# Second feed-forward product of a two-layer trunk: one chain for its loads, moved residual rows, earlier statistics

## The chip, the cores and the metric

One core of a Trainium2 chip runs the whole program. The metric is the device time in microseconds (us) of one execution; several runs are taken and their median is used. The engines are TensorE (PE in the profile; PEld is its weight load), VectorE (DVE), ScalarE (ACT), GpSimd (POOL) and SyncE (SP, which issues nearly all DMA transfers).

## The reference

Two layers; each has a token mixer (latent attention in layer 0, RWKV-7 in layer 1) with memory attention beside it, and then a squared-ReLU feed-forward block:

```
x = layer_norm(ALPHA * x + mix, ln1_g[i], ln1_b[i])
ff = square(relu(x @ w_ff1[i])) @ w_ff2[i]          # 1024x1024 @ 1024x4096, then @ 4096x1024
x = layer_norm(ALPHA * x + ff, ln2_g[i], ln2_b[i])
```

All of it is f32 with 1024 tokens of width 1024. The change lies in the product with `w_ff2` and in the last `layer_norm`.

## The kernel before, in words

Each f32 operand is split into a high part (ScalarE, line 143) and a low part (VectorE, line 144), and each product is three matmuls of 128x128 by 128x512: high-high, high-low, low-high. Both feed-forward products use a Strassen-Winograd scheme: matrices are cut into quarters, and seven smaller products are taken of quarters and their sums and differences. The first product (in `out_and_ff`) writes the hidden quarters A11, A12, A22 and the sums S1 to S4 to DRAM (`h_d`, line 1480), 128 rows per block p = 0..15. It keeps the operand T4 in a pool on the right side of SBUF (lines 1464 and 1465) until its last matmuls.

`second_product` (line 1554) reads them back with the quarters of `w_ff2` in five stretches:

1. A11 x B11 into the PSUM tiles X (`ps_y`) and A12 x B21 into Y (`ps_z`). Steps 0 and 1 hold one block p each and take both weight quarters in one load; steps 2 to 8 hold two blocks (p = 2, 4, ... 14) and need four loads of 512 KB: A11, B11, A12, B21. B21 goes to the kept tile `D_` (`dka` for p < 8, `dkb` for the rest). A step of two blocks has 48 matmuls.
2. S2 and S1 with sums of weights, two blocks a step, five loads a step (lines 1685 to 1690); three weight sums per step are VectorE's.
3. S4 x B22, two loads a step.
4. S3 with a weight difference, three loads a step.
5. A22 with the weights kept in `D_`, one load a step.

Between them `out` (lines 1636 and 1638) adds PSUM tiles into the residual rows `R`, eight row tiles of 128x1024. Before that each row tile is loaded from `n_d` (line 1677) and scaled by g1 and b1 (`scale_rows`, lines 171 and 172, on VectorE). The vectors g1, b1, g2, b2 are loaded as broadcast rows (line 1583) into the ring of four `slot` tiles, which the first product uses too.

Loads go through a ring of raw buffers: `raw()` (line 138) takes turns among the pools `wr`, `w4`, `w3`, `w5` and `w5` again (two buffers each, four in w5). Step 0 uses one of `wr` and one of `w4`; the first buffer of `w5`, which is opened on the right side (line 1576), goes to step 1's hidden rows.

The order of instructions on each engine is written by a planner, which simulates the program and issues what is ready, in program order among the ready. `issue_after(ins)` adds an order edge to `ins` for those instructions of its block that run on the engine of `ins`; it adds no wait. In the code before, the blocks at lines 1659, 1669 and 1674 name `ms[0]`, a matmul, and contain DMA issues of SyncE and VectorE operations:

```
ms = product(X, A1, B1, fresh, end)
with self.tc.issue_after(ms[0]):
    nc.sync.dma_start(r, n_d[(i - 1) * P : i * P, :])
    self.scale_rows(r, g1, b1, nc.vector, nc.vector)
```

In the last layer each row tile is normalised when its sum is complete (`finish`), scaled by g2 and b2 (`affine`) and stored; row tile 7 is stored in two halves (`last_layernorm`). `cp` is a scratch tile of the first product that is free in the second.

Of the kernel before, what the change touches and what calls it, by code (L numbers as in the profile page):

```python
# [10 lines left out]
F32 = mybir.dt.float32  # L11
# [9 lines left out]
P = 128  # L21
T = 1024
D = 1024
KT = D // P
H = 512
# [41 lines left out]
class Trunk:  # L67
# [103 lines left out]
        (mul or self.nc.gpsimd).tensor_mul(r, r, g)  # L171
        (add or self.nc.gpsimd).tensor_add(r, r, b)

    def normalise(self, r):
        y, t = self.row_scale(r)
        self.nc.scalar.activation(r, r, AF.Identity, scale=y, bias=t)


    def last_layernorm(self, r, g, b, dst):
        nc = self.nc  # L180
        y, t = self.row_scale(r)
        for i, (c, q) in enumerate(((slice(0, H), nc.sync), (slice(H, D), nc.scalar))):
            nc.scalar.activation(r[:, c], r[:, c], AF.Identity, scale=y, bias=t)
            self.scale_rows(r[:, c], g[:, c], b[:, c], nc.vector, nc.vector)
            q.dma_start(dst[:, c], r[:, c])


    def row_scale(self, r):
        nc, sm = self.nc, self.sm
        small = lambda name: sm.tile([P, 2], F32, name=f"ln2_{name}", bufs=2)[:, 0:1]  # L190
        st = sm.tile([P, 2, 2, 6], F32, name="ln2_st", bufs=2)[:, 0]
        mv = sm.tile([P, 2, 2], F32, name="ln2_mv", bufs=2)[:, 0, :]
        for i in range(2):
            nc.vector.bn_stats(st[:, i, :], r[:, i * H : (i + 1) * H])
        nc.vector.bn_aggr(mv, st)
        xh, y, t = small("h"), small("y"), small("t")
        nc.vector.tensor_scalar(t, mv[:, 1:2], 1e-5, None, op0=ALU.add)
        nc.vector.tensor_scalar(xh, t, -0.5, None, op0=ALU.mult)
        nc.vector.tensor_scalar(t.bitcast(I32), t.bitcast(I32), 1, None, op0=ALU.logical_shift_right)
        nc.vector.tensor_scalar(y.bitcast(I32), t.bitcast(I32), -1, 0x5F3759DF, op0=ALU.mult, op1=ALU.add)  # L200
        for _ in range(3):
            nc.vector.scalar_tensor_tensor(t, y, xh, y, op0=ALU.mult, op1=ALU.mult)
            nc.vector.scalar_tensor_tensor(y, t, 1.5, y, op0=ALU.add, op1=ALU.mult)
        nc.vector.scalar_tensor_tensor(t, mv[:, 0:1], -1.0, y, op0=ALU.mult, op1=ALU.mult)
        return y, t
# [1043 lines left out]
    def out_and_ff(self, layer, res_src, res_dst, last, R=None):  # L1249
        nc, a = self.nc, self.a  # L1250
        n_d = self.dp.tile([T, D], F32, name=f"n_d{layer}")

        h_d = self.dp.tile([7 * NFF // 2 * P, H], F32, name=f"h_d{layer}")
        h_rows = lambda k, p, n=1: h_d[(k * NFF // 2 + p) * P : (k * NFF // 2 + p + n) * P, :]
        A11_, A12_, A22_, S1_, S2_, S3_, S4_ = range(7)
        pool_of = lambda st: lambda name, bufs=1, **k: st.enter_context(self.tc.tile_pool(name=f"{name}{layer}", bufs=bufs, reuse_waits="tile", **k))
        wv = a["w_ff1"][layer].rearrange("(k p) f -> p k f", p=P)
        quad = lambda t: t.rearrange("p (a b) -> p a b", b=P)
        T0, T1 = slice(0, H), slice(H, T)
        with ExitStack() as s:  # L1260
            pool = pool_of(s)
            cp = pool("cp").tile([P, 2, H], F32, name="cpair")
            pst = pool("pstr", 2, space=PSUM, side="right")
# [7 lines left out]
            with ExitStack() as s1:  # L1271
# [70 lines left out]
                with ExitStack() as s2:  # L1342
# [47 lines left out]
                    if R is None:  # L1390
                        K1 = self.Xh.t[1], self.Xl.t[1]
                        R = Halves(new(0, F32), new(1, F32))
# [152 lines left out]
                        final(*held)  # L1545
                    held = (p, w, A) + m
                final(*held)
            self.second_product(layer, res_dst, last, n_d, h_rows, s, pool_of, pst, slot)
            self.wrs = [self.wr]

    def second_product(self, layer, res_dst, last, n_d, h_rows, s, pool_of, pst, slot):
        nc, a = self.nc, self.a
        A11_, A12_, A22_, S1_, S2_, S3_, S4_ = range(7)
        pool = pool_of(s)
# [18 lines left out]
        w5 = pool("w5", 4, side="right")  # L1576
        self.wrs, self.rn = [self.wr, w4], 1

        def rows(i):
            out = []  # L1580
            for j in range(2):
                t = slot(F32)
                nc.sync.dma_start(t, a["rows"][i + j : i + j + 1, :].broadcast_to([P, D]))
                out.append(t)
            return out

        def hidden(k, p, n=2):
            t = two(self.raw(), n)
            nc.sync.dma_start(t, h_rows(k, p, n).rearrange("(n p) t -> p n t", p=P))
            return t  # L1590

        def weight(i, j, p, n=2, t=None):
            t = two(self.raw(), n) if t is None else t
            nc.sync.dma_start(t, wv[i][:, p : p + n, j * H : (j + 1) * H])
            return t

        def ring(homes):
            while True:
                yield from homes

        def operand(t, home):
            z = [x[:, : t.shape[1], :] for x in home]
            self.split(*z, t)
            return z
# [15 lines left out]
        def product(ps, A, B, fresh, end):  # L1620
            return [block(ps, t, [(A, B)], fresh, end) for t in range(4)]
# [11 lines left out]
        def out(ps, t, tt, cs, fresh):  # L1633
            r = R[:, tt, cs]
            if fresh:
                nc.vector.scalar_tensor_tensor(r, r, ALPHA, ps[t], op0=ALU.mult, op1=ALU.add)
            else:
                nc.vector.tensor_add(r, r, ps[t])

        steps = range(0, N, 2)  # L1640
        home, gate = ring(full), []

        for i, (p, n) in enumerate([(0, 1), (1, 1)] + [(p, 2) for p in steps[1:]]):
            fresh, end = i == 0, p == steps[-1]
            if n == 1:

                t = two(self.raw())
                for j, k in enumerate((A11_, A12_)):
                    nc.sync.dma_start(t[:, j, :], h_rows(k, p))
                w = two(self.raw())  # L1650
                nc.sync.dma_start(w, a["w_ff2"][layer, 2 * p * P : 2 * (p + 1) * P, c0].rearrange("(i p) d -> p i d", p=P))
                za = operand(t, [two(slot()) for _ in range(2)] if i == 0 else next(home))
                zb = operand(w, [two(x) for x in self.split_pair()])
                (A1, B1), (A2, B2) = ([[x[:, j : j + 1, :] for x in z] for z in (za, zb)] for j in range(2))
            else:
                A1, B1 = operand(hidden(A11_, p), next(home)), operand(weight(0, 0, p), next(home))
                A2, (B2, t) = operand(hidden(A12_, p), next(home)), (next(home), D_(p, 2))

                with self.tc.issue_after(gate.pop(0)):
                    weight(1, 0, p, t=t)  # L1660
                B2 = operand(t, B2)
            ms = product(X, A1, B1, fresh, end)
            gate.append(ms[0])
            if end:
                for t in range(4):
                    out(X, t, t, c0, True)
            product(Y, A2, B2, fresh, end)
            if i == 0:
                with self.tc.issue_after(ms[0]):
                    g1, b1 = rows(4 * layer)  # L1670
                self.wrs = [self.wr, w4, w3, w5, w5]
            else:
                r = R[:, i - 1, :]
                with self.tc.issue_after(ms[0]):
                    if i == 1:
                        weight(1, 0, 0, t=D_(0, 2))
                    nc.sync.dma_start(r, n_d[(i - 1) * P : i * P, :])
                    self.scale_rows(r, g1, b1, nc.vector, nc.vector)
        for t in range(4):
            out(Y, t, t, c0, False)  # L1680

# [1 line left out]
        for p in steps:  # L1683
            end = p == steps[-1]
            t11, t12, t22 = weight(0, 0, p), weight(0, 1, p), weight(1, 1, p)
            nc.vector.tensor_sub(t11, t12, t11)
            nc.vector.tensor_sub(t22, t22, t11)
            A, B = operand(hidden(S2_, p), next(home)), operand(t22, next(home))
            A2, B2 = operand(hidden(S1_, p), next(home)), operand(t11, next(home))
            nc.vector.tensor_sub(D_(p, 2), D_(p, 2), t22)  # L1690
            product(X, A, B, False, end)
            if end:
                for t in range(4):
                    out(X, t, t, c1, True)
            product(Y, A2, B2, p == 0, end)
# [11 lines left out]
        def affine(tt):  # L1707
            self.scale_rows(R[:, tt, :], g2, b2, nc.vector, nc.vector)
            nc.sync.dma_start(res_dst[tt * P : (tt + 1) * P, :], R[:, tt, :])
# [2 lines left out]

        def finish(tt):
            if last and tt == KT - 1:
                self.last_layernorm(R[:, tt, :], g2, b2, res_dst[tt * P : (tt + 1) * P, :])
            elif last:
                self.normalise(R[:, tt, :])
                affine(tt)
            elif tt % 2:
                self.normalise2(pair(tt - 1))  # L1720

# [8 lines left out]
                finish(i - 1)  # L1730
        for t in range(4):
            out(X, t, 4 + t, c1, False)

        k = 2 if last else 6
        ops = []
# [160 lines left out]
```

## Time and profile before

| | |
|---|---|
| runs (3) | 2732.3 us median, 2723.94 to 2739.67 |
| profiled execution | 2742.62 us, span 2740.8 |
| PE busy | 2580.5 us (94%) |
| DVE busy | 1805.5 us (66%) |
| ACT busy | 1264.6 us (46%) |
| granted TensorE clock, mean | 0.967 |
| DMA queue q1 | 359.25 MB, 38.6% of 16 engines' span |

The profiled execution is one run, seen by the hardware profiler; rows of its trace add up to its own time. Busy shares are means over the span. The second product of layer 0 runs from about 885 to 1225 us, that of layer 1 from about 2396 us to the end.

### The profile page before, as it was taken

What the parts mean: (1) busy time and instruction counts of PE and PEld (TensorE: products, weight loads), DVE (VectorE), ACT (ScalarE), POOL (GpSimd) and SP (SyncE); (2) the same over time, 40 slices, a digit from 0 to 9 for tenths busy, and PEclk for the clock granted to TensorE, in tenths of its full rate; (3) what the DMA queues carried; (4) which work ended last, traced back from release to release, by engine and by line L of the source; (5) the groups of instructions that cost most, each with busy time, mean ns of one, the idle gap of its engine ahead of it and who ended that gap; (6) DMA issues with size and microseconds to landing.
All of it is one profiled execution on the core that took longest, in us unless ns stands there. A gap on an engine that the chain in (4) does not pass through costs nothing.

```text
span 2740.8 us, 41038 instructions
## 1 busy us (share of the span) xinstructions
PE 2580.5 (94%) x15709; PEld 2085.7 (76%) x15709; DVE 1805.5 (66%) x3195; ACT 1264.6 (46%) x2242; POOL 428.0 (16%) x703
## 2 busy tenths in 40 slices
PE   8999998999999799999989999888998999979998
PEld 7877776778888588887877777666776888858886
DVE  5566766586656676675356566677769666667677
ACT  4465555254444233357344444666527444423343
POOL 0012232000000000002354453454400000000000
PEclk9999999999999899999999999989999999989999
DMA  4100003235445867535521221213114544486661
GB/s 166 56 28 14 9 20 109 88 108 181 146 150 182 315 209 223 184 125 209 193 85 51 72 76 63 93 48 127 59 51 142 177 150 154 158 331 216 218 233 65
DMA packets 233732, 362.13 MB, mean 132 GB/s; under 512 B 14336, under 2 KB 113024, under 8 KB 233536
## 3 DMA queue, kind: packets, MB, share of 16 engines
q1 hardware_dynamic: 233392, 359.25, 38.6%
q8 instruction: 124, 2.03, 0.3%
q14 instruction: 72, 0.59, 0.1%
q10 hardware_dynamic: 144, 0.26, 0.0%
HBM read 254.86 MB, written 104.60 MB: 131 GB/s over the span
## 4 chain that ended last, share of the span: by engine, by line
PE 79%; DVE 10%; DMA 4%; ACT 3%; issue 2%; POOL 1%; SPq 0%; DVEq 0%; POOLq 0%; ACTq 0%
PE ps_f L1288 20%; PE ps_y L1613 12%; PE ps_z L1613 8%; PE ps_in L149 4%; PE ps_in L150 4%; PE ps_in L151 4%; PE ps_o L645 2%; PE ps_pt L636 2%; PE ps_o L149 2%; PE ps_o L150 2%; PE ps_o L151 2%; PE ps_s L611 1%; PE ps_ga L1036 1%; PE ps_s L613 1%; PE ps_s L612 1%
## 5 line engine op out<-in xcount | busy, mean ns | idle before, releaser
L143 ACT CAST Xh<-wraw 128x1024 fp32r<-128x1024 f32 (+1 forms) x138 | 139.2, 1037 | 238.4 <-PE ps_z L1613 72.0
L149 PE MATMUL ps_in<-Xh,whi 128*128 128x512 f32 x480 | 197.6, 414 | 13.3 <-ACT whi L143 9.4
L150 PE MATMUL ps_in<-Xl,whi 128*128 128x512 f32 x480 | 195.2, 407 | 0.8 <-DVE Xl L144 0.8
L151 PE MATMUL ps_in<-Xh,wlo 128*128 128x512 f32 x480 | 194.2, 405 | 0.0
L144 DVE TENSOR_TENSOR Xh<-wraw,Xh 128x1024 fp32r<-128x1024 f32 x115 | 137.6, 1221 | 57.9 <-ACT Xh L143 57.5
L143 ACT CAST Xl<-wraw 128x1024 fp32r<-128x1024 f32 x103 | 104.8, 1050 | 146.7 <-issue 46.1
L144 DVE TENSOR_TENSOR Xl<-wraw,Xl 128x1024 fp32r<-128x1024 f32 x103 | 123.5, 1220 | 50.0 <-ACT Xl L143 49.5
L144 DVE TENSOR_TENSOR wlo<-wraw,whi 128x1024 fp32r<-128x1024 f32 (+3 forms) x93 | 107.1, 1153 | 65.4 <-ACT whi L143 64.9
L143 ACT CAST whi<-wraw 128x1024 fp32r<-128x1024 f32 (+3 forms) x93 | 88.3, 953 | 105.7 <-PE ps_in L150 37.9
L149 PEld LDWEIGHTS ps_in<-Xh,whi 128*128 128x128 f32 x480 | 93.2, 194 | 35.3 <-ACT whi L143 9.4
L626 POOL TENSOR_TENSOR E<-E,l 128x768 f32<-128x768 f32 (+5 forms) x60 | 83.8, 1399 | 201.6 <-DVE l L624 101.3
L1288 PE MATMUL ps_f<-Xh,N 128*128 128x512 f32 x320 | 106.8, 398 | 4.9 <-ACT N L143 2.1
L695 POOL MEMSET wraw<- 128x1 f32 x2 | 0.2, 98 | 698.0 <-DVE wraw L1727 697.9
L150 PEld LDWEIGHTS ps_in<-Xl,whi 128*128 128x128 f32 x480 | 93.1, 194 | 20.1 <-DVE Xl L144 1.3
L151 PEld LDWEIGHTS ps_in<-Xh,wlo 128*128 128x128 f32 x480 | 92.4, 193 | 20.3 <-issue 1.1
L623 ACT ACTIVATE E<-ps_s,mx,SC 128x128 f32<-128x128 f32 (+7 forms) x96 | 79.4, 831 | 51.0 <-DVE mx L621 24.5
L1288 PE MATMUL ps_f<-TB,N 128*128 128x512 f32 x384 | 91.9, 389 | 0.1
L1613 PE MATMUL ps_y<-Xh 128*128 128x512 f32 x384 | 90.0, 389 | 0.0
L1613 PE MATMUL ps_z<-Xh 128*128 128x512 f32 x384 | 89.6, 389 | 0.0
L1613 PE MATMUL ps_z<-Xl 128*128 128x512 f32 x384 | 89.3, 389 | 0.0
L1613 PE MATMUL ps_y<-Xh,Xh 128*128 128x512 f32 x360 | 85.4, 391 | 0.0
L1288 PEld LDWEIGHTS ps_f<-TB,N 128*128 128x128 f32 x384 | 72.0, 188 | 15.4 <-ACT N L143 0.5
(522 smaller groups left out, 7014.5 us busy)
## 6 DMA issues: line engine op xcount, KB each, us to landing
wraw<-in_w_ff_dram SPq DMA_DIRECT2D x182, 512.0 KB, 4.4
wraw<-h_d SPq DMA_DIRECT2D x108, 512.0 KB, 4.2
h_d<-slot SPq DMA_DIRECT2D x128, 256.0 KB, 2.1
h_d<-tr SPq DMA_DIRECT2D x64, 256.0 KB, 2.0
wraw<-in_w_in_dram SPq DMA_DIRECT2D x31, 512.0 KB, 4.0
lo_d<-l_st SPq DMA_DIRECT2D x36, 256.0 KB, 2.3
rkv_d<-rkv_st SPq DMA_DIRECT2D x36, 256.0 KB, 2.3
rkv<-rkv_d SPq DMA_DIRECT2D x24, 384.0 KB, 3.7
```

Of the source, the lines that this page charges most:

```text
L143: h = self.nc.scalar.copy(hi, src)
L144: l = self.nc.vector.tensor_sub(lo, src, f32(hi))
L149: mm(ps, wh, xh, start=first, stop=False)
L150: mm(ps, wh, xl, start=False, stop=False)
L151: mm(ps, wl, xh, start=False, stop=last)
L611: nc.tensor.matmul(o, qh[:, isl], kh, start=True, stop=False)
L623: nc.scalar.activation(E3[:, g, :], S[:, g * w0 : g * w0 + n], AF.Exp, bias=mx[:, g : g + 1], scale=SC[:, i : i + 1], accum_out=l[:, g : g ...
L626: nc.gpsimd.tensor_mul(E3, E3, l[:, :, None].broadcast_to([P, nh, n]))
L636: nc.tensor.transpose(pt[:, j, :], E3[:, g, (j0 + j) * P : (j0 + j + 1) * P], self.ident)
L645: nc.tensor.matmul(po[64 * hd : 64 * hd + 64, i4 * P : (i4 + 1) * P], V[:, j, (2 * pr + hd) * 64 : (2 * pr + hd + 1) * 64], pts[hd][:, j, ...
L1288: yield nc.tensor.matmul(ps, A[x][:, k, :], B[y][:, k, :], start=fresh and k == 0 and i == 0, stop=k == 3 and i == 2, skip_group_check=True)
L1613: m = nc.tensor.matmul(ps[t], A[x][:, u, t * P : (t + 1) * P], B[y][:, u, :], start=fresh and i == u == j == 0, stop=end and i == last_ an ...
```

## The change

All loads of `second_product` go through a new helper `load`, which queues each behind the load before it, in the order of the program text. The residual rows are loaded and scaled from step 3 of the first stretch on, one per step, and two in the second stretch. The vectors g1 and b1 come after step 2. In the last layer, the statistics of the right halves of row tiles 4 to 7 are taken after the fourth stretch, into `cp`, and row tile 6 is scaled and stored after row tile 7.

```diff
+    def row_scale(self, r, st=None):
...
+        halves = range(2 if st is None else 1)
+        st = sm.tile([P, 2, 2, 6], F32, name="ln2_st", bufs=2)[:, 0] if st is None else st
+        for i in halves:
             nc.vector.bn_stats(st[:, i, :], r[:, i * H : (i + 1) * H])
...
+        queue = [None]
+        def load(dst, src):
+            with ExitStack() as st:
+                if queue[0] is not None:
+                    st.enter_context(self.tc.issue_after(queue[0]))
+                queue[0] = nc.sync.dma_start(dst, src).ins
...
         def hidden(k, p, n=2):
             t = two(self.raw(), n)
-            nc.sync.dma_start(t, h_rows(k, p, n).rearrange("(n p) t -> p n t", p=P))
+            load(t, h_rows(k, p, n).rearrange("(n p) t -> p n t", p=P))
...
+        def residual(t):
+            load(R[:, t, :], n_d[t * P : (t + 1) * P, :])
+            self.scale_rows(R[:, t, :], g1, b1, nc.vector, nc.vector)
...
-                A2, (B2, t) = operand(hidden(A12_, p), next(home)), (next(home), D_(p, 2))
-
-                with self.tc.issue_after(gate.pop(0)):
-                    weight(1, 0, p, t=t)
-                B2 = operand(t, B2)
-            ms = product(X, A1, B1, fresh, end)
-            gate.append(ms[0])
+                A2 = operand(hidden(A12_, p), next(home))
+                B2 = operand(weight(1, 0, p, t=D_(p, 2)), next(home))
+            product(X, A1, B1, fresh, end)
...
             if i == 0:
-                with self.tc.issue_after(ms[0]):
-                    g1, b1 = rows(4 * layer)
                 self.wrs = [self.wr, w4, w3, w5, w5]
-            else:
-                r = R[:, i - 1, :]
-                with self.tc.issue_after(ms[0]):
-                    if i == 1:
-                        weight(1, 0, 0, t=D_(0, 2))
-                    nc.sync.dma_start(r, n_d[(i - 1) * P : i * P, :])
-                    self.scale_rows(r, g1, b1, nc.vector, nc.vector)
+            if i == 2:
+                g1, b1 = rows(4 * layer)
+                weight(1, 0, 0, t=D_(0, 2))
+            if i >= 3:
+                residual(i - 3)
...
             nc.vector.tensor_sub(D_(p, 2), D_(p, 2), t22)
+            if 2 <= p <= 4:
+                residual(5 + p // 2)
...
             if last and tt == KT - 1:
-                self.last_layernorm(R[:, tt, :], g2, b2, res_dst[tt * P : (tt + 1) * P, :])
+
+                self.last_layernorm(R[:, tt, :], g2, b2, res_dst[tt * P : (tt + 1) * P, :], stats[:, 3])
+                affine(tt - 1)
             elif last:
-                self.normalise(R[:, tt, :])
-                affine(tt)
+                self.normalise(R[:, tt, :], stats[:, tt - 4] if tt >= 4 else None)
+                if tt != KT - 2:
+                    affine(tt)
...
+        if last:
+            stats = cp[:, 0, 0:48].rearrange("p (t i s) -> p t i s", t=4, i=2)
+            for t in range(4):
+                nc.vector.bn_stats(stats[:, t, 1, :], R[:, 4 + t, c1])
```

`rows`, `weight` and the two single loads of steps 0 and 1 use `load` in the same way.

## Rows read from the trace of the kernel before

**Rows 1.** Waits of TensorE, whole span: in total, times, longest.

```profile
PE ps_y L1613 <- ACT Xh L143: 31.0, 2, 16.6
```

**Rows 2.** Timeline of TensorE, head of layer 0's second product: start, us, instruction.

```profile
895.75 0.39 PE L1613 MATMUL ps_z<-whi,slot 128*128 128x512 f32 x1
910.57 0.79 PE L1613 MATMUL ps_y<-whi,Xh 128*128 128x512 f32 x1 [14.44 <-ACT Xh L143]
...
936.17 5.69 PE L1613 MATMUL ps_z<-Xl,Xh 128*128 128x512 f32 x16 [1.66 <-DVE Xh L144]
941.70 3.56 PE L1613 MATMUL ps_y<-Xh,Xh 128*128 128x512 f32 x15
```

**Rows 3.** Chain of work that ended last, second stretch of layer 0.

```profile
1001.70 5.44 PE ps_y L1613 x24
...
1023.46 5.44 PE ps_y L1613 x24
```

**Rows 4.** Windows, TensorE alone: length, busy (count), clock, DMA share, GB/s.

```profile
896.10:941.60 45.50, 27.32 (x97) 0.74 0.93 360
2407.10:2446.95 39.85, 21.18 (x81) 0.79 1.00 393
```

**Rows 5.** Timeline of TensorE, head of layer 1's second product.

```profile
2406.76 0.39 PE L1613 MATMUL ps_z<-whi,slot 128*128 128x512 f32 x1
...
2440.21 4.83 PE L1613 MATMUL ps_z<-Xh,Xl 128*128 128x512 f32 x20 [1.73 <-DVE Xh L144]
...
2447.02 3.28 PE L1613 MATMUL ps_z<-Xl,Xh 128*128 128x512 f32 x13 [0.17 <-DVE Xh L144]
```

**Rows 6.** Windows, all engines (PE, PEld, DVE, ACT, POOL), the wait and after.

```profile
896.10:910.60 14.50, 0.06 (x2) 0.03 (x1) 8.88 (x10) 1.04 (x1) 0.00 (x0) 0.60 1.04 412
910.60:918.70 8.10, 8.10 (x24) 6.49 (x25) 3.63 (x3) 3.15 (x3) 0.00 (x0) 0.66 1.04 404
```

**Rows 7.** Timeline of SyncE's queue, layer 0.

```profile
870.95 0.46 SPq L1589 DMA_DIRECT2D wraw<-h_d  x1
...
893.58 5.42 SPq L1677 DMA_DIRECT2D R<-n_d  x5
899.38 1.51 SPq L1649 DMA_DIRECT2D wraw<-h_d  x2
```

**Rows 8.** Landing times of lines 1649, 1651 and 1677, in this order.

```profile
DMA to landing us min/median/max: 2.5/5.8/9.4
...
DMA to landing us min/median/max: 3.6/4.8/6.3
...
DMA to landing us min/median/max: 8.9/9.5/10.7
```

**Rows 9.** Timeline of TensorE, the last reader of T4 in layer 0.

```profile
891.66 0.39 PE L1288 MATMUL ps_f<-T,wlo 128*128 128x512 f32 x1
```

**Rows 10.** Timeline of VectorE and ScalarE, layer 0.

```profile
901.52 0.69 DVE L1531 TENSOR_TENSOR tr<-tr,slot 128x512 f32<-128x512 f32 x1
...
903.22 6.16 DVE L171 TENSOR_TENSOR R<-R,slot 128x1024 f32<-128x1024 f32 x5 [1.01 <-DMA R<-n_d]
...
909.47 1.04 ACT L143 CAST Xh<-wraw 128x1024 fp32r<-128x1024 f32 x1 [15.94 <-DMA wraw<-h_d]
...
913.26 1.23 DVE L144 TENSOR_TENSOR Xl<-wraw,Xl 128x1024 fp32r<-128x1024 f32 x1
```

**Rows 11.** Timeline of VectorE, second stretch of layer 0.

```profile
1026.60 1.22 DVE L1690 TENSOR_TENSOR dkb<-dkb,wraw 128x1024 f32<-128x1024 f32 x1
```

**Rows 12.** Windows, all engines, unbroken part of layer 0's first stretch.

```profile
936.20:1023.30 87.10, 87.10 (x377) 71.99 (x377) 58.54 (x57) 31.13 (x32) 0.00 (x0) 0.98 0.63 199
```

**Rows 13.** Chain of work that ended last, end of the kernel.

```profile
2729.15 1.14 DVE R L171
2730.29 0.60 DVE ln_st L194
2730.89 1.12 DVE R L172
```

More of the change, by code (lines that the diff above doesn't have):

```diff
@@ L172, in scale_rows, with normalise, last_layernorm @@
         (add or self.nc.gpsimd).tensor_add(r, r, b)
-    def normalise(self, r):
-        y, t = self.row_scale(r)
+    def normalise(self, r, st=None):
+        y, t = self.row_scale(r, st)
         self.nc.scalar.activation(r, r, AF.Identity, scale=y, bias=t)
-    def last_layernorm(self, r, g, b, dst):
+    def last_layernorm(self, r, g, b, dst, st):
         nc = self.nc
-        y, t = self.row_scale(r)
+        y, t = self.row_scale(r, st)
         for i, (c, q) in enumerate(((slice(0, H), nc.sync), (slice(H, D), nc.scalar))):
@@ L185, in last_layernorm @@
             q.dma_start(dst[:, c], r[:, c])
-    def row_scale(self, r):
+    def row_scale(self, r, st=None):
         nc, sm = self.nc, self.sm
         small = lambda name: sm.tile([P, 2], F32, name=f"ln2_{name}", bufs=2)[:, 0:1]
-        st = sm.tile([P, 2, 2, 6], F32, name="ln2_st", bufs=2)[:, 0]
         mv = sm.tile([P, 2, 2], F32, name="ln2_mv", bufs=2)[:, 0, :]
-        for i in range(2):
+        halves = range(2 if st is None else 1)
+        st = sm.tile([P, 2, 2, 6], F32, name="ln2_st", bufs=2)[:, 0] if st is None else st
+        for i in halves:
             nc.vector.bn_stats(st[:, i, :], r[:, i * H : (i + 1) * H])
@@ L1547, in out_and_ff, with second_product @@
                 final(*held)
-            self.second_product(layer, res_dst, last, n_d, h_rows, s, pool_of, pst, slot)
+            self.second_product(layer, res_dst, last, n_d, h_rows, s, pool_of, pst, slot, cp)
             self.wrs = [self.wr]
-    def second_product(self, layer, res_dst, last, n_d, h_rows, s, pool_of, pst, slot):
+    def second_product(self, layer, res_dst, last, n_d, h_rows, s, pool_of, pst, slot, cp):
         nc, a = self.nc, self.a
@@ L1582, in rows @@
                 t = slot(F32)
-                nc.sync.dma_start(t, a["rows"][i + j : i + j + 1, :].broadcast_to([P, D]))
+                load(t, a["rows"][i + j : i + j + 1, :].broadcast_to([P, D]))
                 out.append(t)
@@ L1593, in weight @@
             t = two(self.raw(), n) if t is None else t
-            nc.sync.dma_start(t, wv[i][:, p : p + n, j * H : (j + 1) * H])
+            load(t, wv[i][:, p : p + n, j * H : (j + 1) * H])
             return t
+        def residual(t):
+            load(R[:, t, :], n_d[t * P : (t + 1) * P, :])
+            self.scale_rows(R[:, t, :], g1, b1, nc.vector, nc.vector)
         def ring(homes):
@@ L1640, in second_product @@
         steps = range(0, N, 2)
-        home, gate = ring(full), []
+        home = ring(full)
         for i, (p, n) in enumerate([(0, 1), (1, 1)] + [(p, 2) for p in steps[1:]]):
@@ L1648, in second_product @@
                 for j, k in enumerate((A11_, A12_)):
-                    nc.sync.dma_start(t[:, j, :], h_rows(k, p))
+                    load(t[:, j, :], h_rows(k, p))
                 w = two(self.raw())
-                nc.sync.dma_start(w, a["w_ff2"][layer, 2 * p * P : 2 * (p + 1) * P, c0].rearrange("(i p) d -> p i d", p=P))
+                load(w, a["w_ff2"][layer, 2 * p * P : 2 * (p + 1) * P, c0].rearrange("(i p) d -> p i d", p=P))
                 za = operand(t, [two(slot()) for _ in range(2)] if i == 0 else next(home))
```

## The prediction

> **What bounds the kernel now.** TensorE is by far the busiest engine of the page's table, so only its idle or slowed stretches can be won. The list of what TensorE waited for comes first: its longest entry is 31.0 us in two waits, both in the second feed-forward product, behind a ScalarE cast (line 143, the high half of an operand) [rows 1]. No other entry of the list's head lies in code that the change touches. So the question is what happens at the head of that product, once per layer.
>
> TensorE's timeline of layer 0 shows it. The last matmul of step 0 starts at 895.75, the first of step 1 at 910.57; a later piece begins after a gap of 1.66 at 936.17, and from 941.70 on nothing interrupts it [rows 2]. Undisturbed, 24 matmuls take 5.44 us, 0.2267 each [rows 3]. Between 895.98 (895.75 + 0.23) and 941.70, 45.72 us, it did 96 matmuls (the window's x97 counts the one that reaches into it) [rows 2, 4], worth 96 x 0.2267 = 21.76. Lost: 23.96 us. In layer 1 step 0 ends at 2406.99 and the unbroken part begins at 2447.02: 40.03 us for 80 matmuls (x81, counted in the same way) [rows 4, 5], worth 18.13. Lost: 21.90. Together 45.9 us: 31.0 are the two long waits, the rest is lower clock (0.74 and 0.79 were granted over the two stretches [rows 4]) and shorter gaps.
>
> Why is step 1 late? During the wait the DMA engines are full, at 412 GB/s [rows 6], so that 512 KB take 0.524 / 0.41 = 1.28 us of them. SyncE's timeline shows what they carry: hidden rows of step 2 issued at 870.95, five residual rows from 893.58 to 899.0, and only then, at 899.38, the hidden rows that step 1 wants [rows 7]. A residual row takes 9.5 us to land here [rows 8]. By the code these rows should follow a matmul of their own step, ms[0]; but that helper orders only instructions of the named one's engine, and the loads are SyncE's. The trace bears it out: five were issued before step 1's first matmul. The order that the old code asks for was never in force, and the new chain, whose links are all SyncE's, is a real change of order.
>
> **The change part by part, per layer.**
>
> *The chain's first price.* Step 1's hidden rows go to the first buffer of w5, which by the code lies where T4 lay. T4's last reader starts at 891.66 [rows 9], so the buffer is free near 891.9, whatever the order. The loads behind it in the chain, some of which leave at 870 to 892 today, now wait for 892; but then only stores are in front of them. Two halves of hidden rows at 0.32 of SyncE each land 2.5 us after issue at best, the weights 3.6 at best [rows 8]: hidden rows landed 892.1 + 0.3 + 0.64 (half of 1.28) + 2.5 = 895.5, cast (1.04 [rows 10], 1.05 with its start) at 896.6; weights issued by 893.1, landed 896.7, cast 897.8, low half on VectorE (1.23 [rows 10]) 899.0. Step 0 still ends at 895.98, so TensorE idles 3.0 us where it idled 14.6.
>
> *Clock.* After the long wait 24 matmuls took 8.1 us [rows 6] where 5.4 would do: 2.7 lost. After the gap of 1.73 in layer 1, 20 matmuls took 4.83 where 20 x 0.2267 + 0.16 (the last one's tail) = 4.69 would do: 0.14 lost; after layer 0's gap, 16 took 5.53 for 3.63: 1.9 lost [rows 2, 5]. A 3 us gap lies between 0.1 and 2.7; I take 1.5, nearer to the short gaps.
>
> *Step 2.* Its four loads (2 MB) follow directly: the first pair is landed by 896.7 + 2 x 1.28 = 899.3, or 901.2 with three 256 KB stores of the last block between (0.64 each); cast and low half make 903.5. Step 1's 24 matmuls run until 899.0 + 5.44 + 1.5 = 905.9. VectorE also has six sums of the last block (0.69 each [rows 10], 4.1) and four low halves: 892.5 + 4.1 + 4.9 = 901.5. Covered; bounds 0 to 4 us (the six sums on top), I take 1 for VectorE's order.
>
> *Row vectors.* The two of them (1 MB) and one more weight block go behind step 2. The second waits for a slot that the last block's stores leave; today the last of its sums starts at 901.52 [rows 10], so it goes by 904 at the latest and holds back step 3: landed by 904 + 4 x 1.28 + 2.5 = 911.6, wanted at 905.9 + 10.9 = 916.8. Hidden; if not, it costs up to those 2 us of its late issue.
>
> *Residual rows.* Eight loads leave the head of the queue and return one per step from step 3: 2.5 MB per step, 5 x 1.28 = 6.4 us of DMA in a step of 48 matmuls, 10.88. VectorE per step: four low halves, 4.9, and a mul and an add (6.16 / 5 = 1.23 each [rows 10]), 7.4 of 10.88. Two rows fall into the second stretch, where a step already costs VectorE seven such operations, 8.6; with the row 11.1 of 10.88. VectorE's lead covers it: at 1026.60 it works on the first weight block of dkb (p = 8) [rows 11], while TensorE began p = 4 at 1023.46 (two steps after p = 0 at 1001.70) [rows 3]. Without that lead the two rows cost 2 x 2.5. I take 0.
>
> *Later loads.* After 947 TensorE does not wait in the product today, so the chain can win nothing there; in its first unbroken 87 us VectorE is busy 58.54 of 87.10 us and DMA 0.63 [rows 12]. I take 0; the last but one rival prices the other end.
>
> *The end.* Row 6's mul and add (1.14 and 1.12 on the chain of waits) stand between row 7's sum and its normalising [rows 13]. Moved behind row 7 they free 2.26 us and then stand at the end themselves, with a 512 KB store where a 256 KB one ended the kernel, 0.64 more. If the mul fits into VectorE's wait for ScalarE, the end is 0.5 to 1 earlier; if not, 0.6 later. One bn_stats (0.60) stands there too [rows 13]: the early halves save nothing if it is the half summed last, 0.6 if not. I take 0 for all of it.
>
> Sum: 45.9 - 2 x (3.0 + 1.5 + 1.0) = 34.9, say 35 us. The profiled execution took 2742.6 (span 2740.8), so 2707.6; it is 10.3 above the median of the runs, 2732.3, and against that the forecast is 2697.
>
> **Two rules weighed.** In the wait the queue moved 412 GB/s [rows 6]. The Trainium skill, "DMA: Bandwidth & Descriptors", section Specifications, gives one core's HBM limit as about 358 GB/s. By that figure a 512 KB load would take an estimated 1.46 us and the seven loads up to step 2 would come 1.3 us later in each layer; the trace lies above the page, and the measurement decides. The same page of the Trainium skill, section Rules for kernel authors, says to issue a DMA early and to wait for it late. By that rule the chain is wrong where it holds loads back until 892; the first rival is this case.
>
> **The rivals.**
>
> *Late start (0.13).* All of step 2 is held until 892, and today some of its loads leave near 870 [rows 7]. If the last block's sums go first on VectorE (4.1 us), step 1 begins 3 later than above, step 2 waits 4, and the clock costs 2.7: a loss of 6 + 4 + 2.7 = 12.7 per layer, a gain of 45.9 - 25.4 = 20.5, time 2712. For it: VectorE works in a written order. Against: the planner that writes it knows of the buffer.
>
> *Residual rows take the place of the wait (0.09).* A row's scaling stands in VectorE's order ahead of a low half and waits there for its load, as L171 begins behind a load at 903.22 [rows 10]. Two us in six steps of two layers give 24 back: 2721. Against: each row's load now stands behind its own step's operands.
>
> *Slower (0.07).* In the second and fourth stretch SyncE stands at a load whose ring buffer is not free, all later loads stand behind it, and their landing is exposed: 4.3 us (between 2.5 and 6.3 [rows 8]) at up to 16 steps in each layer. It decides from 35 / 32 = 1.1 us a step. At every second step it costs 69: 2732 + 69 - 35 = 2766. For it: three to five loads a step there. Against: ten buffers hold two steps and more, and VectorE's lead [rows 11].
>
> *The chain changes nothing (0.01)*, if SyncE's order were as today: 2732.
>
> **How the numbers follow.** The forecast has 0.70, with its own range 2684 to 2712 (its loss 0 to 9 a layer, and some 6 us between runs). 0.5% is 13.7 us, about what a measurement of this kernel can tell from no change. Faster: the forecast and most of the late start, 0.81; same 0.11; slower 0.08. The range 2682 to 2726 takes in the first two rivals.
>
> **What would show it.** After the change: SyncE issues step 1's hidden rows within 1 us of T4's last matmul; no residual load leaves before step 3's operands; TensorE's wait for step 1 is 2 to 6 us; row 6's mul and add follow row 7's sum. I am wrong if that wait is over 8 us, if waits appear after step 3, or if the later stretches take more than 5.44 us per 24 matmuls.

## The result and the profile after

The changed kernel takes 2698.2 us (median; 2694.9 to 2701.3) beside 2734.7 for the kernel before on the same chip: ratio 0.9872, interval 0.9838 to 0.9906. Its profiled execution took 2700.9.

TensorE is busy 2564.5 of 2699.1 us. The list of its waits over the whole span begins with (in total, times, longest; in this kernel line 1628 is the second product's matmul, line 1588 its `load`, line 1482 a store of the first product):

```profile
PE ps_y L1628 <- ACT whi L143: 9.7, 2, 5.2
PE ps_y L1146 <- DVE W L1163: 9.6, 15, 1.5
```

The two waits of 31.0 us in total [rows 1] are down to 9.7, and they are now for the cast of a weight (`whi`), not of hidden rows (`Xh`); the second entry, 9.6 in 15 short waits, lies in other code. TensorE's timeline at the two heads (start, us, instruction), and the windows from the end of step 0 to the unbroken part (length, then PE, PEld, DVE, ACT, POOL, granted clock, DMA share, GB/s):

```profile
891.22 0.39 PE L1290 MATMUL ps_f<-T,wlo 128*128 128x512 f32 x1
...
895.30 0.39 PE L1628 MATMUL ps_z<-whi,slot 128*128 128x512 f32 x1
...
900.25 2.07 PE L1628 MATMUL ps_y<-whi,Xh 128*128 128x512 f32 x4 [4.56 <-ACT whi L143]
...
908.03 5.60 PE L1628 MATMUL ps_y<-Xh,Xh 128*128 128x512 f32 x24
913.47 5.60 PE L1628 MATMUL ps_z<-Xl,Xh 128*128 128x512 f32 x24
...
2379.49 0.39 PE L1628 MATMUL ps_z<-whi,slot 128*128 128x512 f32 x1
...
2385.06 2.07 PE L1628 MATMUL ps_y<-whi,Xh 128*128 128x512 f32 x4 [5.18 <-ACT whi L143]
...
2392.81 5.60 PE L1628 MATMUL ps_y<-Xh,Xh 128*128 128x512 f32 x24
```

```profile
895.50:908.00 12.50, 7.94 (x25) 6.23 (x25) 5.63 (x5) 5.23 (x5) 0.00 (x0) 0.73 0.91 308
...
2379.70:2392.80 13.10, 7.92 (x25) 6.22 (x25) 4.97 (x5) 5.23 (x5) 0.00 (x0) 0.74 0.87 292
```

Read as in [rows 2, 5]: step 0 ends at 895.53 (895.30 + 0.23), step 1 runs from 900.25 to 908.03, and from there each 24 matmuls take 5.44. Lost in layer 0: 12.50 - 5.44 = 7.06 us; in layer 1, from 2379.72, 13.09 - 5.44 = 7.65. That is 14.7 where the kernel before lost 45.9: the heads give 31.2. The profiled executions differ by 41.7, so 10.5 more lie elsewhere. The count of matmuls finds 8.3 of them in layer 1's token mixer, which the change doesn't touch (the table at the end of the experiments), and 1.2 ahead of the first matmul (9.38 before, 8.22 after); the last 1.0 is spread over the other stages.

SyncE's timeline shows the new order of issue:

```profile
891.64 0.32 SPq L1588 DMA_DIRECT2D wraw<-h_d  x1
892.05 0.41 SPq L1482 DMA_DIRECT2D h_d<-tr  x1
892.51 0.42 SPq L1588 DMA_DIRECT2D wraw<-h_d  x1
892.99 0.49 SPq L1588 DMA_DIRECT2D wraw<-in_w_ff_dram  x1
893.57 0.47 SPq L1482 DMA_DIRECT2D h_d<-slot  x1
894.14 0.85 SPq L1482 DMA_DIRECT2D h_d<-tr  x2
895.04 1.06 SPq L1588 DMA_DIRECT2D wraw<-h_d  x1
900.44 0.38 SPq L1588 DMA_DIRECT2D wraw<-in_w_ff_dram  x1
901.89 1.09 SPq L1588 DMA_DIRECT2D slot<-in_rows_dram  x2
...
906.18 1.54 SPq L1588 DMA_DIRECT2D dka<-in_w_ff_dram  x1
...
908.23 1.28 SPq L1588 DMA_DIRECT2D R<-n_d  x1
```

Step 1's hidden rows leave at 891.64 where they left at 899.38 [rows 7]; the first residual row (`R<-n_d`) leaves at 908.23, behind step 3's operands. Between the two halves of the hidden rows and the weights' landing, four 256 KB stores of the last block (line 1482) pass.

### The profile page after: what moved, and what is told of

Same layout as the page of the kernel before. It is cut to its first block, busy times and chain, and to the rows that moved or that the text cites. A ratio compares the mean times of both kernels' runs of the same rounds, so it can differ in the third digit from the quotient of the medians.

```text
span 2699.1 us, 40995 instructions
## 1 busy us (share of the span) xinstructions
PE 2564.5 (95%) x15709; PEld 2073.5 (77%) x15709; DVE 1803.9 (67%) x3195; ACT 1266.7 (47%) x2242; POOL 429.8 (16%) x703
## 4 chain that ended last, share of the span: by engine, by line
PE 81%; DVE 9%; ACT 3%; DMA 3%; issue 2%; POOL 1%; SPq 0%; DVEq 0%; ACTq 0%; POOLq 0%
PE ps_f L1290 20%; PE ps_y L1628 13%; PE ps_z L1628 10%; PE ps_in L149 4%; PE ps_in L150 4%; PE ps_in L151 4%; PE ps_o L647 2%; PE ps_pt L638 2%; PE ps_o L149 2%; PE ps_o L150 2%; PE ps_o L151 2%; PE ps_ga L1038 1%; PE ps_s L613 1%; PE ps_s L615 1%; PE ps_s L614 1%
```

## The experiments

Losses below are a head's length less that of its matmuls undisturbed (300 in layer 0, 68.0 us; 600 in layer 1, 136.0), all read from matmul starts.

**Is it the order of issue?** The changed kernel without the links between loads; the moved residual rows stay moved.

```diff
-            with ExitStack() as st:
-                if queue[0] is not None:
-                    st.enter_context(self.tc.issue_after(queue[0]))
-                queue[0] = nc.sync.dma_start(dst, src).ins
+            nc.sync.dma_start(dst, src)
```

> The changed kernel without the chain's order edges; the residual rows stay where the change put them in the text. Chain theory: SyncE again issues kept weights and residual rows as soon as their memory is free, ahead of step 1's hidden rows; the two heads lose 15 to 24 us each again, 2715 to 2735 us. Rival (moving the rows in the text is enough): heads lose about 7 us each as in the changed kernel, 2700 us.

Measured: 2736.4 us, ratio to before 1.0017 (1.0003 to 1.0031). TensorE's waits and SyncE's timeline:

```profile
PE ps_y L1625 <- ACT Xh L143: 30.3, 2, 15.1
```

```profile
893.33 4.12 SPq L1585 DMA_DIRECT2D R<-n_d  x4
...
898.47 1.78 SPq L1585 DMA_DIRECT2D wraw<-h_d  x2
```

The old wait is back whole, and so is the old order: four residual rows leave ahead of step 1's hidden rows although the program text has them two steps later. The heads lose 23.2 and 25.3 us; the second and the median lie a little past the upper end of what was expected. The text's order alone gains nothing; without the links the change is worth nothing.

**One layer at a time.** e2 has the new second product in layer 0 alone, e3 in layer 1 alone.

```diff
-            self.second_product(layer, ...)
+            (self.second_product_old if layer else self.second_product)(layer, ...)
...
```

The lines left out are the old second product, added under the other name; e3 has the two names the other way round.

> The change's second product in layer 0 alone, the old one in layer 1. Between the two heads the trace of the changed kernel gained another 10 us in layer 1's token mixer, where the planner wrote another order. Theory (that order is worth 10 us): 17 at layer 0's head and 10 in the mixer, 2734.7 - 27 = 2708 us, and the mixer's length in the trace as in the changed kernel within 2 us. Rival (the 10 us are run-to-run variation): 2718 us, mixer's length anywhere between the two.

> The old second product in layer 0, the change's in layer 1; the mixer's order is that of the kernel before. Theory: only layer 1's head gains, 14 us, 2734.7 - 14 = 2720 us, and the mixer takes as long as in the kernel before within 2 us. Rival (variation): the mixer's length differs from before by 5 us or more although its order is the same.

Measured: e2 2715.2, ratio 0.9931 (0.9909 to 0.9953), a gain of 16.9; e3 2718.7, 0.9944 (0.9923 to 0.9966), a gain of 13.4. Their profiles lose 6.0 and 8.1 us at the new head and keep one old wait each. The gains add up to 30.2, close to the heads' 31.2, with nothing over for the mixer. e2's mixer, 668.7 us, fits its theory and its rival alike; its median lies nearer to the rival's 2718 than to 2708. e3 decides: it has before's code up to layer 1's mixer and still spends 669.7 us there, not 675.6. So the theory that another order in layer 0 changes the mixer fell.

**The end alone.** The kernel before with the early statistics and with row 6's scaling behind row 7.

```diff
...
+                affine(tt - 1)
...
+                if tt != KT - 2:
+                    affine(tt)
...
+            stats = cp[:, 0, 0:48].rearrange("p (t i s) -> p t i s", t=4, i=2)
+            for t in range(4):
+                nc.vector.bn_stats(stats[:, t, 1, :], R[:, 4 + t, c1])
```

> The kernel before with the edits at the end alone: the early halves of the statistics and row 6 scaled behind row 7 in the text. Theory: within 2 us of before, 2732, since the planner fills VectorE's gaps with row 6's mul and add all the same, as it did in the changed kernel's trace. Rival (the end is worth what the heads don't explain, some 3 us of 34): 2729.

Measured: 2733.9, ratio 1.0004 (0.9987 to 1.002). No gain to be seen, as the sum had it.

**Where do the residual rows and vectors belong?** The links stay; the vectors go behind step 0, and a residual row to each step from 1 (with the kept weights of p = 0 at step 1).

```diff
             if i == 0:
+                g1, b1 = rows(4 * layer)
                 self.wrs = [self.wr, w4, w3, w5, w5]
...
-            if i >= 3:
-                residual(i - 3)
+            else:
...
+                residual(i - 1)
```

> The changed kernel with the chain, but the row vectors and the residual rows at their old places in the text (row vectors after step 0, one residual row per step from step 1 on). Theory (the order that the chain fixes must also be the right one): step 1's hidden rows stand behind the second row vector, which waits for the last block's stores; step 1 begins 3 to 6 us later than in the changed kernel, the heads lose 11 to 14 us each instead of 7.3, 2706 to 2712 us. Rival (any fixed order does): 2698 us.

Measured: 2701.3 (2698.8 to 2710.2), ratio 0.9902 (0.9879 to 0.9925). The list of TensorE's waits, and SyncE's timeline ahead of step 1's hidden rows, which follow at 896.09:

```profile
PE ps_y L1628 <- ACT whi L143: 15.9, 2, 8.1
```

```profile
895.66 0.33 SPq L1588 DMA_DIRECT2D slot<-in_rows_dram  x1
```

The second vector stands in front, as the theory had it. The waits grow from 9.7 to 15.9, the losses to 11.0 and 10.2: the mechanism is there, at or just under the low end of what was expected, and the median lies under the theory's 2706. By the heads it costs 6.4 us; the medians of the two kernels, measured in different runs, don't separate them.

**What is left of the wait.** Step 1's first buffer lies where T4 lay. Here the ring of five pools begins two steps later, so that steps 1 and 2 use the buffers that are free before:

```diff
-            if i == 0:
-                self.wrs = [self.wr, w4, w3, w5, w5]
             if i == 2:
+                self.wrs = [self.wr, w4, w3, w5, w5]
```

> The changed kernel with the loads of steps 1 and 2 kept on the pools wr and w4, which are free before T4 is (the longer ring begins with step 3). Theory (the 4.7 and 5.6 us that TensorE still waits at step 1 come from w5's buffer lying where T4 lay): the wait at step 1 falls below 1 us and the head's loss from 7 to under 2 us per layer, 2698 - 11 = 2687 us, give or take another order in the mixer. Rival (the last block's stores and sums are what is late): the wait stays above 3 us at step 1 or comes back at step 2, 2695 us or more.

Measured: 2685.1 (2676.7 to 2687.8), ratio 0.982 (0.9794 to 0.9845). TensorE's and SyncE's timelines and the window of step 1:

```profile
895.26 0.39 PE L1628 MATMUL ps_z<-whi,slot 128*128 128x512 f32 x1
895.49 1.07 PE L1628 MATMUL ps_y<-whi,Xh 128*128 128x512 f32 x4
...
900.93 5.60 PE L1628 MATMUL ps_y<-Xh,Xh 128*128 128x512 f32 x24
```

```profile
870.48 0.94 SPq L1588 DMA_DIRECT2D wraw<-h_d  x2
871.45 0.43 SPq L1588 DMA_DIRECT2D wraw<-in_w_ff_dram  x1
```

```profile
895.50:900.90 5.40, 5.40 (x25) 1.00 0.97 294
```

Step 1's loads leave at 870, 21 us earlier; there is no gap, the granted clock stays at 1.00 (2.4 GHz), and both heads take exactly 68.0 and 136.0. What the change had left at the heads, 14.7 us, all came of the late buffers (those of steps 1 and 2 were moved together); by the medians, of different runs, e4 is 13 us under the changed kernel.

**Do the buffers need the links?** e4's buffers without them.

> The early buffers for steps 1 and 2, without the chain's order edges. Theory (the chain is needed for step 3 on, which stands behind the kept weights and the residual rows): no wait at step 1, but one of 3 to 8 us at step 3, 2692 to 2702 us. Rival (buffers were the whole cause and the chain is not needed): no wait over 1 us, 2685 us.

Measured: 2716.0, ratio 0.995 (0.9932 to 0.9967), slower than either theory had it. TensorE's and SyncE's timelines:

```profile
913.73 2.11 PE L1625 MATMUL ps_y<-Xl,Xl 128*128 128x512 f32 x8 [2.08 <-ACT Xl L143]
...
939.62 7.79 PE L1625 MATMUL ps_y<-Xh,Xh 128*128 128x512 f32 x24 [9.21 <-ACT Xh L143]
```

```profile
896.57 1.65 SPq L1585 DMA_DIRECT2D R<-n_d  x2
...
913.33 0.32 SPq L1585 DMA_DIRECT2D R<-n_d  x1
...
928.91 0.94 SPq L1585 DMA_DIRECT2D wraw<-h_d  x2
```

Step 1 is in time. But six of the eight residual rows leave from 896.57 to 913.33, among the operands of the next steps, and after them four stores of the last block. TensorE waits 2.1 us at step 3, and its long wait, 9.2 us now, stands at 939.62, in step 4, behind hidden rows that leave at 928.91. That these rows cause it is the plain reading, with e1 beside it; it was not tried by itself. With the moved rows in all four kernels, the buffers alone give 16.7 us of median against before, the links alone 36.4 (the changed kernel), both together 47.0, and neither (e1) is 4.4 slower.

**The changed kernel again, for the mixer.** Not a line is changed.

> The changed kernel once more, beside the next one on the same chip. Theory: 2698 us within 4, and its mixer's length in the trace differs from the first profile's by a few us although nothing is changed. Rival (the mixer's length is fixed by its order): within 1 us of the first profile.

Measured: 2700.1 (2696.9 to 2705.0), ratio 0.9878 (0.984 to 0.9916); its mixer takes 660.6 us where the first profile of the same kernel had 667.3. Windows over that stage of before, after and this run (columns as above):

```profile
1395.80:2071.40 675.60, 613.93 (x6000) 481.69 (x5999) 453.34 (x1188) 328.81 (x830) 283.33 (x563) 0.93 0.22 73
```

```profile
1377.90:2045.20 667.30, 601.86 (x6003) 471.75 (x6002) 453.77 (x1188) 329.06 (x830) 285.61 (x563) 0.95 0.22 74
```

```profile
1380.00:2040.50 660.50, 594.38 (x6004) 465.94 (x6002) 453.44 (x1187) 328.82 (x829) 285.53 (x563) 0.96 0.23 74
```

The work of VectorE, ScalarE and GpSimd takes the same time within 2.3 us; TensorE's busy time falls with the same number of matmuls, 613.9, 601.9, 594.4 (its weight loads likewise), and the granted clock rises with it. The stage's length goes with the clock of the execution.

**Row 6 on GpSimd.** e4, with row 6's mul and add on GpSimd.

```diff
-                affine(tt - 1)
+                affine(tt - 1, nc.gpsimd)
```

> The changed kernel with the early buffers for steps 1 and 2, and row 6's last mul and add on GpSimd, so that VectorE has nothing between row 7's sum and its normalising. Theory: 13 us faster than the changed kernel by the heads, as with the early buffers alone, and 2.3 us less from the last matmul to the end: 2683 us. Rival (GpSimd is so slow, or slows VectorE beside it so much, that row 6 ends last): 2686 us or more, with GpSimd on the last chain.

Measured: 2686.3, ratio 0.9819 (0.9785 to 0.9852), no better than e4. From the start of row 7's last sum to the end of the span: 12.43 us, 12.37 in e4. Timelines of GpSimd and VectorE:

```profile
2666.64 2.34 POOL L171 TENSOR_TENSOR R<-R,slot 128x1024 f32<-128x1024 f32 x1 [658.79 <-ACT R L176]
...
2669.06 2.34 POOL L172 TENSOR_TENSOR R<-R,slot 128x1024 f32<-128x1024 f32 x1
...
2669.23 2.19 DVE L204 SCALAR_TENSOR_TENSOR ln_t<-ln_y,ln_h 128x1 f32<-128x1 f32 x1
...
2671.64 0.22 DVE L204 SCALAR_TENSOR_TENSOR ln_t<-ln_y,ln_h 128x1 f32<-128x1 f32 x1
```

Row 7's small operation of 128x1 took 2.19 us beside GpSimd's add instead of 0.22: the time taken off VectorE came back as contention. The median is the rival's; but GpSimd is not on the last chain, it lengthens VectorE's part of it.

**Row 6 really last.** e4, with an order edge behind row 7's last add.

```diff
...
-                affine(tt - 1)
+                with self.tc.issue_after(end):
+                    affine(tt - 1)
```

> The early buffers, and row 6's mul, add and store truly behind row 7's on VectorE, by an order edge; in the changed kernel the planner had left them between row 7's sum and its normalising. Theory (my working of the end): row 7's stores leave 2.3 us sooner, row 6's mul and add then take 2.3 at the end, and its 512 KB store lands 0.6 later than a 256 KB one: from the start of row 7's sum to the end of the span 12.9 us where it was 12.3; median 2685, as with the early buffers alone. Rival (only row 7's own chain counts at the end): 10.0 us, median 2683.

Measured: 2685.1, ratio 0.9821 (0.9804 to 0.9837). VectorE's and SyncE's timelines:

```profile
2664.52 0.69 DVE L1652 SCALAR_TENSOR_TENSOR R<-R,ps_y 128x512 f32<-128x512 f32 x1 [0.92 <-PE ps_y L1629]
...
2671.87 1.22 DVE L171 TENSOR_TENSOR R<-R,slot 128x1024 f32<-128x1024 f32 x1
2673.12 1.23 DVE L172 TENSOR_TENSOR R<-R,slot 128x1024 f32<-128x1024 f32 x1
2674.38 0.33 SPq L1718 DMA_DIRECT2D out_dram<-R  x1
```

The end takes 13.27 us from that sum (2677.79 - 2664.52), 0.9 more than in e4 where 0.6 was expected: row 6's mul, add and store now close the kernel. A row written last is worse here than one that fills gaps; the medians, e4's 2685.1 again, don't show it.

The profiles side by side, with the mixer (matmuls 6900 to 12900) taken out of the span:

| kernel | head 0 | head 1 | mixer | span less mixer |
|---|---|---|---|---|
| before | 92.0 | 158.1 | 675.6 | 2065.2 |
| e1 no links | 91.2 | 161.3 | 663.5 | 2068.3 |
| e5 end alone | 89.5 | 158.0 | 669.8 | 2065.6 |
| e3 layer 1 | 92.6 | 144.1 | 669.7 | 2050.6 |
| e7 buffers, no links | 82.0 | 150.6 | 663.4 | 2049.7 |
| e2 layer 0 | 74.0 | 157.8 | 668.7 | 2047.9 |
| e6 rows early | 79.0 | 146.2 | 663.6 | 2044.8 |
| after | 75.1 | 143.7 | 667.3 | 2031.8 |
| e8 after again | 74.4 | 143.9 | 660.6 | 2034.5 |
| e9, e4 + GpSimd | 68.0 | 136.0 | 657.9 | 2020.7 |
| e10, e4 + row 6 last | 68.0 | 136.0 | 657.1 | 2020.7 |
| e4 links and buffers | 68.0 | 136.0 | 665.7 | 2020.3 |

Without the mixer the kernels, e6 apart, fall into groups that agree within 3.1 us, and the heads explain most of the steps between them. From before to after this difference is 33.3: 31.2 of the heads, and 1.2 of the rest at the start. e6 lies 13.0 above after, of which the heads are 6.4; the rest is spread over stages that differ between executions of one kernel too. One example: behind a short wait at 1185.44 in layer 0's product, 24 matmuls take 7.20 us in e6 and 7.20 in e8 at the same place, but 5.59 in after, the same kernel as e8.

## Why the prediction was right, and where it was not

*The cause.* Right, and shown, as far as it is the order of issue: step 1's operands stood behind other loads, in an order that the old code's edges did not enforce. Taking the links away (e1) brings back both the order and the wait. Not shown is that the five residual rows do it alone. The kernel before also issues eight kept weight blocks (`dka`, `dkb`) from 882.49 to 892.57, an estimated 10 us of the DMA engines by the prediction's 1.28 us each. While the rows leave, SyncE waits for these blocks to land. From its timeline, and from the list of its waits from 840 to 960:

```profile
887.02 2.25 SPq L1594 DMA_DIRECT2D dkb<-in_w_ff_dram  x3
```

```profile
SPq L1677 <- DMA dkb<-in_w_ff_dram: 2.8, 3, 1.0
```

The chain holds both back, and no run parts them.

*The idle before step 1: 3.0 foreseen, 4.7 and 5.3 measured* (900.25 - 895.53; 2385.06 - 2379.72). The term for the landing is the one that was mis-sized. ScalarE's timeline:

```profile
896.03 1.04 ACT L143 CAST Xh<-wraw 128x1024 fp32r<-128x1024 f32 x1 [5.84 <-DMA wraw<-h_d]
...
899.15 1.04 ACT L143 CAST whi<-wraw 128x1024 fp32r<-128x1024 f32 x1 [2.07 <-DMA wraw<-in_w_ff_dram]
```

The hidden rows were cast at 896.03 (895.5 foreseen), the weights at 899.15 instead of 896.7. They were issued at 892.99, as foreseen, and their cast began 6.2 us later, not after the 3.6 of the shortest landing that I had taken [rows 8]; the last block's stores run beside them. These stores are the likely reason; it was not tried alone. The median of these landings, 4.8, would have been the better choice. The sign "2 to 6 us" was met.

*Clock: 1.5 foreseen, 2.3 measured.* Step 1's 24 matmuls take 7.78 (908.03 - 900.25) and 7.75, not 5.44, at a granted clock of 0.73 and 0.74 over the windows. The term belonged nearer to the 2.7 after the long wait than to the short gap.

*Step 2: 1.0 foreseen, 0 measured.* But a thing happened there that the prediction had only in a rival, and elsewhere. SyncE's waits, from 885 to 935:

```profile
SPq L1588 <- DMA h_d<-tr: 4.3, 1, 4.3
```

Step 2's first weight load stood 4.3 us, until 900.44, for a buffer that a store was still reading, and every later load stood behind it. The cover was step 1's own lateness: what it held back was wanted only at 908. The price of a chain on one queue is thus seen here once, free of charge; in the later stretches, where the slower rival put it, no wait of TensorE is added. One of 1.5 us stands at 1180.34 in layer 0; the kernel before has it too, 1.6 at 1197.58, against the prediction's "After 947 TensorE does not wait in the product today".

*The residual rows and the vectors: 0 foreseen, 0 measured* in the place they have. e6 shows what hides them: two steps of distance less, and the losses at the heads rise by 3.9 and 2.5 us.

*The end: 0 foreseen and measured, but by a wrong picture.* "Moved behind row 7 they free 2.26 us" did not occur. The chain of waits of the changed kernel at its end:

```profile
2686.77 0.70 DVE R L1651
2687.49 0.70 DVE cpair L196
2688.19 1.12 DVE R L171
2689.31 0.12 DVE ln_mv L197
2689.43 1.14 DVE R L172
```

Row 6's mul and add (L171, L172) still stand between row 7's sum (L1651) and its normalising, among its statistics (L196, L197), as in [rows 13]; the planner that orders VectorE fills its gaps with them whatever the program text says. The early statistics save nothing either: one half (`bn_stats`) stands behind the sum before and after. From row 7's sum to the end 12.36 us pass, 12.34 before. The sign "row 6's mul and add follow row 7's sum" was met by the letter, and was too weak to see this.

*The sum.* 45.9 - 14.7 = 31.2 against 34.9: 4.1 too little for the idle time and 1.6 for the clock, less the 2.0 put down for step 2. That the forecast 2697 lies only 1.2 from 2698.2 is luck: the medians of two sets of executions also differ, and the changed kernel's gain measured 36.4 here and 32.5 when it was run again (e8). Subtracting the profile's 10.3 us above the median was the right way to keep its slow mixer out.

*The rivals.* "Late start" named the right residue, step 1 held until T4 is read, at 12.7 a layer; it is 7.1 and 7.7, and e4 removes it whole. Its wait of 4 us at step 2 did not come. Residual rows in place of the wait, the slower case and "nothing" did not occur.

Still open: which loads ahead of step 1 cost how much, and why one execution grants the mixer 0.93 of the clock and another 0.97. Best version run: e4, 2685.1 (e10 has the same median).

## What to carry to other kernels

When a step waits for its operands while the DMA engines are full, read from the issuing queue's timeline what went ahead of them; an edge in the code is no evidence that the order is in force. Once the order is right, the next limit is the buffer: a load at the head of a chain must not aim at memory whose last reader has just finished, and here moving one line was worth 13 us. Compare stages by matmul count before crediting a change with a difference of the whole span.

## What was not expected of the hardware

GpSimd's add of 128x1024 ran 2.34 us, and beside it VectorE's 128x1 operation on two SBUF tiles ended with it after 2.19 us (0.22 without). The Trainium skill, "SBUF — State Buffer", section "SBUF: two separate sides" (under "Who interferes with whom"), says that VectorE with two SBUF inputs and a GpSimd operation that reads SBUF take a shared port pair in turn, each for a whole instruction; e9's trace agrees: GpSimd's add ends at 2671.40, VectorE's operation at 2671.42. The mixer, the same 6000 matmuls each time, took from 657.1 to 675.6 us by the granted clock of the execution, 18.5 us, about half of what the whole change gives by its medians.
